# Layer 1's up projection as seven block products over all 1024 tokens, with down after it

## The chip, the cores and the metric

One core of a Trainium2 chip runs the whole program. The metric is the device time of one execution in microseconds. The kernel before took 2512.34, 2510.89 and 2510.45 us in three runs, 2510.89 in the median. Engines are named as in the profile: PE (TensorE), DVE (VectorE), ACT (ScalarE), POOL (GpSimd), SP (SyncE, which issues most transfers).

## The reference, cut to what matters

Two layers over 1024 tokens of width 1024. Each has four token mixers side by side, an output projection and a gated FFN with a causal convolution of three taps over the tokens. All in float32.

```python
def conv_ffn(h, w_up, conv_w, conv_b, w_down):
    a, b = jnp.split(h @ w_up, 2, axis=-1)            # w_up: 1024 x 5632
    a = causal_dwconv(a, conv_w) + conv_b.astype(a.dtype)
    return (jax.nn.gelu(a, approximate=True) * b) @ w_down   # 2816 x 1024

def hybrid_layer(x, ...):
    h = rms_norm(x, g_pre_mix)
    p = h @ w_in
    ...
    y = jnp.concatenate([y_a, y_b, y_c, y_d], axis=-1).astype(dt)   # pool, retention, gating, deltanet
    x = x + rms_norm(y @ w_out, g_post_mix)
    h = rms_norm(x, g_pre_ffn)
    x = x + rms_norm(conv_ffn(h, w_up, conv_w, conv_b, w_down), g_post_ffn)
    return x
```

The deltanet mixer is a recurrence over chunks of 64 tokens: a triangular system is solved in each chunk, then the state is carried on.

## The kernel before

**Numbers.** Every matmul operand is a pair of fp32r tiles: hi, a cast by ACT, and lo, the difference by DVE (`split`, and `unit` for weights, L182 and L183). A product is three matmuls: hi hi, hi lo, lo hi. `a_unit` multiplies one weight tile of 1024 x 128 with the transposed rows of 512 tokens: 8 x 3 = 24 matmuls 512 columns wide (L192 to L194). `b_units` is the form with tokens on the output's partitions, 256 columns wide (L213 to L215).

**Tiling.** The tokens go through in two halves h of 512, each in four blocks of 128. A layer is, for each half, `win` (input projection and mixers), `out` (output projection, then `norms`: the residual and the norm ahead of the FFN), and `ffn`. An FFN has 22 blocks f of 128 channels. For each, two units give the two parts of the up projection, ACT and DVE do the convolution, the gelu and the product (L1020 to L1029), and the result g is split. Two blocks f at a time go through `down`: per token block and half of the output, 6 matmuls and an addition to `acc` in SBUF (L997 to L1004). So up and down alternate through the whole FFN, and neither g nor the transposed rows leave SBUF.

**The end of layer 1.** `out` of half 1 is called in the middle of half 0's `ffn`, after 14 of its 22 blocks f (`MID` = 7). Half 1's normed rows are transposed (`to_hT`), half 1's `ffn` follows, and `last_norm` ends the program.

**Order.** The Tile framework schedules the instructions of each engine ahead of time, from its own model of their times and from priorities, and puts in the waits; each engine then runs its queue strictly in that order. In this way the mixers of half 1 in layer 1 are spread among the matmuls of half 0's FFN. The deltanet's second part is, per block of 128 tokens, `dn_solve` (four steps, each some small matmuls and a copy that the next step needs: L854, L862, L871, L877 with L886 and L888) and `dn_scan` (L916 and L923 carry the state, L931 and L934 make the output, then `heads_norm` and the transposes L940). Transfers are nearly all issued by SP, in its queue's order.

Of the kernel before, what the change touches and what calls it, by code (L numbers as in the profile page):

```python
# [19 lines left out]
P = 128  # L20
# [93 lines left out]

class Net:
    up = 0

    def __init__(self, tc, ctx, t, dbg=None):
# [13 lines left out]
        self.pd = pool("pd", 1, space=DRAM)  # L132
        self.setup()

    def setup(self):
# [146 lines left out]
        return g  # L282

    def sumsq(self, x):
        sq = self.px.tile([P, D], BF16, tag="junk", name="sq", bufs=1)
# [4 lines left out]
    def norms(self, raw, hn, gpost, gpre, src, dst):  # L290
        nc = self.nc
        for b in range(NB):
            xb = self.px.tile([P, D], F32, tag="xb", name="xb")
            nc.sync.dma_start(xb, src[b * P:b * P + P])
            if raw is not None:
                r = self.sumsq(raw[b])
                nc.vector.scalar_tensor_tensor(raw[b], raw[b], r, gpost, ALU.mult, ALU.mult)
                nc.vector.tensor_tensor(xb, xb, raw[b], ALU.add)
                nc.sync.dma_start(dst[b * P:b * P + P], xb)
            if gpre is not None:  # L300
                r = self.sumsq(xb)
                nc.vector.scalar_tensor_tensor(hn[b], xb, r, gpre, ALU.mult, ALU.mult)

    def last_norm(self, raw, gpost, src, dst):
        nc = self.nc
        xbs = []
        for b, tag in enumerate(("qf", "kt", "rg", "su")):
            xb = self.pp.tile([P, D], F32, tag=tag, name=f"x{tag}")
            nc.gpsimd.dma_start(xb, src[b * P:b * P + P])
            xbs.append(xb)  # L310
        V = nc.vector
        mk = lambda nm: self.px.tile([P, 1], F32, tag=f"{nm}1", name=nm, bufs=4)
        for b, xb in enumerate(xbs):
            sq = self.px.tile([P, D], BF16, tag="junk", name="sq", bufs=1)
# [630 lines left out]
    def out(self, l, h, y, mid=False, halves=False):  # L945
        self.up = UO
        nc, t = self.nc, self.t
# [31 lines left out]
        self.norms(raw, hn, gpost, gpre, src, dst)  # L979
        return hn  # L980

    def ffn(self, l, h, hT, mid=None):
        self.up = UF
# [73 lines left out]
    def run(self):  # L1057
# [98 lines left out]
```

## Time and profile before

| | |
|---|---|
| median of three runs | 2510.89 us |
| profiled execution, span | 2507.0 us |
| PE busy | 2447.9 us, 98% |
| DVE busy | 1730.2 us, 69% |
| ACT busy | 943.0 us, 38% |
| POOL busy | 234.0 us, 9% |
| PE's share of the chain of waits | 84% |

The program itself took the span, 2507.0 us, from its first instruction to its last in one execution; the times of the runs are from others, and their median is 3.9 us above it. Stages of layer 1 in that execution: half 1's mixers and half 0's FFN up to about 1914 us, `out` of half 1 from 1914 to 2013 us, half 0's remaining FFN and half 1's from there to 2495 us, and the last norm to 2507 us. In a row of a timeline the first number is the start and the second the duration in us; what stands in brackets is idle time ahead of it and what ended it. In a row of groups the numbers behind the bar are the sum in us and the mean of one in ns. In a row by stretches each engine has its busy time and its count, followed by the granted clock of PE, the share of the DMA engines and GB/s.

### The profile page before, as it was taken

What the parts mean: (1) busy time and instruction counts of PE and PEld (TensorE: products, weight loads), DVE (VectorE), ACT (ScalarE), POOL (GpSimd) and SP (SyncE); (2) the same over time, 40 slices, a digit from 0 to 9 for tenths busy, and PEclk for the clock granted to TensorE, in tenths of its full rate; (3) what the DMA queues carried; (4) which work ended last, traced back from release to release, by engine and by line L of the source; (5) the groups of instructions that cost most, each with busy time, mean ns of one, the idle gap of its engine ahead of it and who ended that gap; (6) DMA issues with size and microseconds to landing.
All of it is one profiled execution on the core that took longest, in us unless ns stands there. A gap on an engine that the chain in (4) does not pass through costs nothing.

```text
span 2507.0 us, 35870 instructions
## 1 busy us (share of the span) xinstructions
PE 2447.9 (98%) x13916; PEld 2035.9 (81%) x13916; DVE 1730.2 (69%) x3561; ACT 943.0 (38%) x1417; POOL 234.0 (9%) x318
## 2 busy tenths in 40 slices
PE   8989998999999999899999999989999999999998
PEld 7968987877788987787778898778778988888886
DVE  8895699765655788956665579895556386555556
ACT  6334452432332454342332345333233343323233
POOL 2321103000000022200000002220000000000001
PEclk9999999999999999999999999999999999999999
DMA  5233333322223452232223354222223253422332
GB/s 186 72 90 111 127 137 91 99 85 76 81 93 113 157 177 76 76 102 78 76 76 101 118 169 160 85 76 85 76 85 101 93 172 114 157 93 87 101 101 84
DMA packets 94655, 265.60 MB, mean 106 GB/s; under 512 B 30146, under 2 KB 30466, under 8 KB 93972
## 3 DMA queue, kind: packets, MB, share of 16 engines
q1 hardware_dynamic: 90564, 251.17, 31.0%
q0 software_dynamic: 3344, 11.08, 1.3%
q8 instruction: 110, 1.80, 0.3%
q10 hardware_dynamic: 576, 1.05, 0.1%
q14 instruction: 61, 0.50, 0.1%
HBM read 241.20 MB, written 22.05 MB: 105 GB/s over the span
## 4 chain that ended last, share of the span: by engine, by line
PE 84%; DVE 11%; issue 4%; ACT 1%; DMA 0%; POOL 0%; SPq 0%; DVEq 0%; POOLq 0%; ACTq 0%
PE psg L193 16%; PE psg L194 16%; PE psg L192 15%; PE psg L997 7%; PE psg L998 6%; PE psg L999 6%; PE psg L213 3%; PE psg L214 3%; PE psg L215 3%; DVE pr L811 3%; DVE A L813 2%; DVE wlo L183 1%; PE psh L345 1%; PE psm L871 1%; PE psm L934 1%
## 5 line engine op out<-in xcount | busy, mean ns | idle before, releaser
L193 PE MATMUL psg<-hT,whi 128*128 128x512 f32 x1856 | 739.1, 398 | 1.8 <-DVE hT L349 1.8
L194 PE MATMUL psg<-hT,wlo 128*128 128x512 f32 x1856 | 737.7, 399 | 0.0
L192 PE MATMUL psg<-hT,whi 128*128 128x512 f32 x1856 | 731.0, 394 | 0.1
L182 ACT CAST whi<-raw 128x1024 fp32r<-128x1024 f32 (+1 forms) x383 | 398.0, 1048 | 782.1 <-PE psg L193 316.2
L183 DVE TENSOR_TENSOR wlo<-raw,whi 128x1024 fp32r<-128x1024 f32 (+1 forms) x360 | 442.2, 1235 | 283.1 <-ACT whi L182 276.0
L192 PEld LDWEIGHTS psg<-hT,whi 128*128 128x128 f32 x1856 | 353.5, 190 | 79.7 <-issue 0.2
L193 PEld LDWEIGHTS psg<-hT,whi 128*128 128x128 f32 x1856 | 349.6, 188 | 83.6 <-DVE hT L349 2.6
L194 PEld LDWEIGHTS psg<-hT,wlo 128*128 128x128 f32 x1856 | 349.5, 188 | 75.6 <-issue 0.2
L1004 DVE TENSOR_TENSOR acc<-acc,psg 128x512 f32<-128x512 f32 x312 | 212.7, 686 | 135.9 <-PE psg L999 134.5
L997 PE MATMUL psg<-whi,g 128*128 128x512 f32 x696 | 277.3, 400 | 0.3 <-DVE acc L1004 0.3
L998 PE MATMUL psg<-wlo,g 128*128 128x512 f32 x696 | 273.9, 394 | 0.0
L999 PE MATMUL psg<-whi,g 128*128 128x512 f32 x696 | 273.4, 393 | 0.0
L214 PE MATMUL psg<-wlo,hT 128*128 128x256 f32 (+1 forms) x512 | 150.0, 294 | 8.4 <-DVE wlo L183 8.4
L997 PEld LDWEIGHTS psg<-whi,g 128*128 128x128 f32 x696 | 130.7, 188 | 31.4 <-DVE acc L1004 1.6
L999 PEld LDWEIGHTS psg<-whi,g 128*128 128x128 f32 x696 | 130.8, 188 | 30.3
L998 PEld LDWEIGHTS psg<-wlo,g 128*128 128x128 f32 x696 | 130.9, 188 | 27.3 <-DVE c L1029 0.2
L1029 DVE TENSOR_TENSOR c<-c,psg 128x512 f32<-128x512 f32 x88 | 60.5, 688 | 131.7 <-PE psg L194 125.0
L215 PE MATMUL psg<-whi,hT 128*128 128x256 f32 (+1 forms) x512 | 149.4, 293 | 0.0
L213 PE MATMUL psg<-whi,hT 128*128 128x256 f32 (+1 forms) x512 | 146.9, 291 | 1.3 <-DVE rqk L490 1.1
L213 PE MATMUL psg<-whi,y 128*128 128x256 f32 x512 | 141.8, 282 | 1.7 <-ACT raw L975 0.9
L215 PE MATMUL psg<-whi,y 128*128 128x256 f32 x512 | 142.8, 282 | 0.0
L214 PE MATMUL psg<-wlo,y 128*128 128x256 f32 x512 | 142.6, 281 | 0.0
(380 smaller groups left out, 3178.9 us busy)
## 6 DMA issues: line engine op xcount, KB each, us to landing
raw<-in_wU SPq DMA_DIRECT2D x176, 512.0 KB, 3.5
raw<-in_wD SPq DMA_DIRECT2D x88, 512.0 KB, 3.5
raw<-in_wA SPq DMA_DIRECT2D x56, 512.0 KB, 3.6
raw<-in_wO SPq DMA_DIRECT2D x32, 512.0 KB, 3.9
raw<-in_wB SPq DMA_DIRECT2D x24, 512.0 KB, 3.5
xs<-xb SPq DMA_DIRECT2D x24, 512.0 KB, 3.4
xb<-xs SPq DMA_DIRECT2D x20, 512.0 KB, 3.6
raw<-in_wS SPq DMA_DIRECT2D x8, 528.0 KB, 3.6
```

Of the source, the lines that this page charges most:

```text
L182: nc.scalar.copy(hi[:, :n], raw[:, :n])
L183: eng.tensor_tensor(lo[:, :n], raw[:, :n], hi[:, :n].bitcast(F32), ALU.subtract)
L192: nc.tensor.matmul(ps, a[0], b[0], start=first, stop=False)
L193: nc.tensor.matmul(ps, a[0], b[1], start=False, stop=False)
L194: nc.tensor.matmul(ps, a[1], b[0], start=False, stop=last)
L213: self.nc.tensor.matmul(ps[:, :width], h0, hi[:, s], start=k == 0, stop=False)
L214: self.nc.tensor.matmul(ps[:, :width], h0, lo[:, s], start=False, stop=False)
L215: self.nc.tensor.matmul(ps[:, :width], h1, hi[:, s], start=False, stop=k == len(hT) - 1)
L997: nc.tensor.matmul(ps, hi[:, tb], us[i][0][:, s], start=i == 0, stop=False)
L998: nc.tensor.matmul(ps, hi[:, tb], us[i][1][:, s], start=False, stop=False)
L999: nc.tensor.matmul(ps, lo[:, tb], us[i][0][:, s], start=False, stop=i == len(g0) - 1)
L1004: V.tensor_tensor(acc[b][:, s], acc[b][:, s], ps, ALU.add)
```

## The change

Only layer 1's FFN and what surrounds it changes (`FULL = (1,)`).

- **Plain part.** For f = 0 to 7, half 0's up projection is made as before (`plain_up`): five blocks ahead of `out` of half 1 and three behind it. g goes to DRAM (`gD`) unsplit.
- **Normed rows to DRAM.** `norms` of layer 1 also writes the normed rows of both halves to DRAM (`hnD`).
- **Three memory layouts.** `phase` closes one set of SBUF pools and opens another: one for the mixers, one for the up projection, one for down.
- **Operands.** `build` reads a half's normed rows back, transposes them, and makes seven operands (hi and lo each) from the four blocks A11, A12, A21, A22 (token half by half of the 1024 channels): A11, A12, A22, S1, S2, S3, Q4.
- **Seven products.** `up_f` loads both weight tiles of a block f, forms seven 512 x 128 weight operands by four additions on DVE (L1111) and seven splits (L1106, L1107), and makes seven products of 4 x 3 = 84 matmuls (L1090 to L1092) in place of eight. Sums of products are kept in PSUM or made by ACT and DVE. For f = 0 to 7 it runs on half 1 alone (256 columns), for f = 8 to 21 on both halves (512 columns). g goes to DRAM.
- **Down.** `down_full` then reads g back and runs over all eight token blocks, in one group of two f and five groups of four. The last group ends each token block with its norm (`end_block`).

A line of the program before is found 18 to 20 lines further down in the changed one up to `dn_scan` (L854 is L874, L862 L882, L871 L891, L877 L897, L886 and L888 L906 and L908, L916 L936, L931 and L934 L951 and L954, L940 L960).

**The tail of the deltanet on PE, before.** The end of one block (L940) and the first two steps of the next (L854, L862); L192 to L194 are half 0's up projection, `x_97` the solve's tile.

```order
L940 MATMUL psm<-ident,tmp 128x128 x2
L854 MATMUL psm<-x_97,LT 32x32 x8
L192 MATMUL psg<-hT_16160,whi 128x512
L193 MATMUL psg<-hT_16162,whi 128x512
L194 MATMUL psg<-hT_16160,wlo 128x512
...
L192 MATMUL psg<-hT_16160,whi 128x512
L862 MATMUL psm<-XT,x_97 32x32 x8
L193 MATMUL psg<-hT_16162,whi 128x512
```

22 matmuls of 512 columns stand between the two steps.

**The same place on PE, after.** The end of one block and the steps of the next.

```order
L954 MATMUL psm<-R_14590,AT 128x64 x2
L960 MATMUL psm<-ident,tmp 128x128 x2
L874 MATMUL psm<-x_100,LT 32x32 x8
L882 MATMUL psm<-XT,x_100 32x32 x8
L891 MATMUL psm<-R_14590,XT 128x128 x4
L897 MATMUL psm<-AT,R_14590 64x128 x4
L906 MATMUL psm<-kt,R_14590 64x64
L908 MATMUL psm<-R_14590,kt 64x64
...
L936 MATMUL psm<-S,tmp 64x64 x8
L951 MATMUL psm<-Sb,qf 64x128 x2
L954 MATMUL psm<-R_14590,AT 128x64 x2
```

The steps now follow one another directly; the up and down matmuls that stood between them have moved behind.

**SP's queue around `build`, after**, with what each row waits for (a name of an engine, or of a transfer queue): g's writes of the plain part (L1026), the last normed rows (L322), the normed rows read back (L1052) and the weights of the first products (L1101).

```order
L1026 DMA gD_109<-c 128x512 [waits DMAHW1_49,DVE_49]
L1101 DMA wraw<-in_wU 128x2x1024 [waits DMAHW2_49,PE_49]
L322 DMA hnD_107<-osu 128x1024 [waits DMAHW3_49,DVE_49]
L1052 DMA hn<-hnD_107 128x1024 [waits DMASW4_49,DMAHW4_49,DMASW2_49,DMASW0_49]
L1052 DMA hn<-hnD_107 128x1024 [waits DMAHW6_49,DMAHW5_49,DMAHW1_49]
L1052 DMA hn<-hnD_107 128x1024 [waits DMASW1_49]
L1052 DMA hn<-hnD_107 128x1024 [waits DMAHW7_49,DMAHW3_49]
```

The rows are read back behind the write of the last of them.

**SP's queue at the start of down, after**: the last writes of g (L1164), g read back (L1177) and the first weights of down (L198).

```order
L1164 DMA gD_109<-c 128x1024 [waits DMAHW4_49,DVE_49,Activation_49]
L1177 DMA graw<-gD_109 128x1024 [waits PE_49]
L1177 DMA graw<-gD_109 128x1024 [waits DMAHW6_49]
L1164 DMA gD_109<-c 128x1024 [waits DMAHW7_49,DVE_49,Activation_49]
L198 DMA raw<-in_wD 128x1024 [waits DMAHW0_49]
L198 DMA raw<-in_wD 128x1024 [waits DMAHW1_49]
```

The first weights of down stand behind the write of the last block's g, which waits for DVE.

The diff, cut to its core:

```diff
+FULL = (1,)
+NPRE, NHALF = 5, 8
...
+    def mix_phase(self):
+        self.phase(("pw", 3), ("pr", NR), ("pa", 4), ("py", 2), ("pt", 5), ("ph", 4), ("pp", 1))
+    def up_phase(self):
+        self.phase(("pv", 2), ("pu", 1), ("pA", 1))
+    def down_phase(self):
+        self.phase(("pw", 6), ("pg", 6), ("pa", 8), ("pr", 2), ("py", 2))
...
                 nc.vector.scalar_tensor_tensor(hn[b], xb, r, gpre, ALU.mult, ALU.mult)
+                if keep is not None:
+                    nc.sync.dma_start(keep[b * P:b * P + P], hn[b])
...
+    def plain_up(self, l, h, fs, hT):
+        for f in fs:
+            c = self.pa.tile([P, HALF], F32, tag="acc", name="c")
+            pa = self.a_unit(self.t["wU"][l, 2 * f], hT)
+            pb = self.a_unit(self.t["wU"][l, 2 * f + 1], hT)
+            with self.tc.high_priority(offset=1500):
+                self.conv_gate(l, h, f, c, pa, pb)
+            self.nc.sync.dma_start(self.gD[l][f, :, h * HALF:h * HALF + HALF], c)
...
+    def build(self, l, h):
...
+            def put(n, src):
+                hi, lo = self.A[n]
+                nc.scalar.copy(hi[:, :, cs], v4(src))
+                V.tensor_tensor(lo[:, :, cs], v4(src), hi[:, :, cs].bitcast(F32), ALU.subtract)
+            put("A11", p00)
+            nc.scalar.copy(a21, p10)
+            V.tensor_tensor(s1, a21, p11, ALU.subtract)
+            put("S1", s1)
+            V.tensor_tensor(s2, s1, p00, ALU.subtract)
+            put("S2", s2)
+            put("A12", p01)
+            V.tensor_tensor(s3, p00, a21, ALU.subtract)
+            put("S3", s3)
+            V.tensor_tensor(q4, s2, p01, ALU.add)
+            put("Q4", q4)
+            put("A22", p11)
...
+    def up_f(self, l, f, halves):
...
+        self.product(X, "A11", w11, cs, True, False)
+        self.product(Z, "S1", wt1, cs, True, False)
+            nc.scalar.copy(p1, X)
+            nc.scalar.copy(p5, Z)
+        self.product(X, "S2", wt2, cs, False, False)
+        self.product(W, "A12", w21, cs, True, True)
+            nc.scalar.copy(u2, X)
+            V.tensor_tensor(p1, p1, W, ALU.add)
+        self.product(X, "S3", wt3, cs, False, False)
+        self.product(Z, "Q4", w22, cs, False, True)
+            V.tensor_tensor(at[:, :, 1], v(p5), v(X), ALU.subtract)
+            V.tensor_tensor(at[:, :, 0], v(Z), v(u2), ALU.subtract)
+        self.product(X, "A22", wt4, cs, False, True)
+            nc.scalar.activation(c, a[:, 2:], AF.Identity, bias=cb, scale=w(2))
...
+        nc.sync.dma_start(self.gD[l][f, :, halves[0] * HALF:halves[0] * HALF + 2 * N], c)
...
-        acc = self.ffn(l, 0, self.to_hT(acc, True), lambda: hn.extend(self.out(l, 1, y, True)))
-        hT = self.to_hT(hn)
-        self.ffn_norm(l, 0, acc)
-        self.ffn_norm(l, 1, self.ffn(l, 1, hT))
+        hT = self.to_hT(acc, True)
+        self.plain_up(l, 0, range(NPRE), hT)
+        self.out(l, 1, y, True)
+        self.plain_up(l, 0, range(NPRE, NHALF), hT)
+        self.up_phase()
+        self.rows(l)
+        self.build(l, 1)
+        for f in range(NHALF):
+            if f == 1:
+                self.build(l, 0)
+            self.up_f(l, f, (1,))
+        for f in range(NHALF, NF):
+            self.up_f(l, f, (0, 1))
+        self.down_phase()
+        self.down_full(l)
```

More of the change, by code (lines that the diff above doesn't have):

```diff
@@ L143, in setup @@
         self.xs = [self.pd.tile([SEQ, D], F32, name=f"xs{i}") for i in range(2 * DEPTH - 1)]
+        self.hnD = [self.pd.tile([SEQ, D], F32, name=f"hnD{i}") for i in range(DEPTH)]
+        self.gD = [self.pd.tile([NF, P, SEQ], F32, name=f"gD{i}") for i in range(DEPTH)]
         self.pm = {}
@@ L288, in sumsq, with norms @@
         return self.rstd(ss, 1, 1.0 / D)
-    def norms(self, raw, hn, gpost, gpre, src, dst):
+    def norms(self, raw, hn, gpost, gpre, src, dst, keep=None):
         nc = self.nc
         for b in range(NB):
-            xb = self.px.tile([P, D], F32, tag="xb", name="xb")
+            xb = self.py.tile([P, D], F32, tag="xb", name="xb")
             nc.sync.dma_start(xb, src[b * P:b * P + P])
@@ L978, in out, with conv_gate @@
         hn = raw if mid else self.acc_tiles()
-        self.norms(raw, hn, gpost, gpre, src, dst)
+        self.norms(raw, hn, gpost, gpre, src, dst, self.hnD[l][h * HALF:h * HALF + HALF] if l in FULL else None)
         return hn
+    def conv_gate(self, l, h, f, c, pa, pb):
+        nc, pf = self.nc, self.pf[l]
+        V, cf = nc.vector, self.state[l]["cf"]
+        w = lambda j: pf[:, PF_CW + 3 * f + j:PF_CW + 3 * f + j + 1]
+        cb = pf[:, PF_CB + f:PF_CB + f + 1]
+        nc.scalar.activation(c, pa, AF.Identity, bias=cb, scale=w(2))
+        if h == 0:
+            nc.scalar.copy(cf[:, f, :], pa[:, 510:512])
+        V.scalar_tensor_tensor(c[:, 1:512], pa[:, 0:511], w(1), c[:, 1:512], ALU.mult, ALU.add)
+        V.scalar_tensor_tensor(c[:, 2:512], pa[:, 0:510], w(0), c[:, 2:512], ALU.mult, ALU.add)
+        if h == 1:
+            V.scalar_tensor_tensor(c[:, 0:2], cf[:, f, :], w(0), c[:, 0:2], ALU.mult, ALU.add)
+            V.scalar_tensor_tensor(c[:, 0:1], cf[:, f, 1:2], w(1), c[:, 0:1], ALU.mult, ALU.add)
+        nc.scalar.activation(c, c, AF.Gelu_apprx_tanh)
+        V.tensor_tensor(c, c, pb, ALU.mult)
@@ new lines, in product @@
+    def product(self, ps, a, b, cs, first, last):
+        nc = self.nc
+        ah, al = self.A[a]
+        for k in range(4):
+            s = slice(k * P, k * P + P)
+            st, sk = first and k == 0, not first
+            nc.tensor.matmul(ps, b[:, 0, s], ah[:, k, cs], start=st, stop=False, skip_group_check=sk)
+            nc.tensor.matmul(ps, b[:, 0, s], al[:, k, cs], start=False, stop=False, skip_group_check=sk)
+            nc.tensor.matmul(ps, b[:, 1, s], ah[:, k, cs], start=False, stop=k == 3, skip_group_check=sk)
@@ new lines, in down_full @@
+    def down_full(self, l):
+        nc, t = self.nc, self.t
+        V = nc.vector
+        gpost = self.bcast(t["gB"][4 * l + 3], "gpost", pool=lambda n: self.py.tile([P, D], F32, tag="gpost", name=n, bufs=1))
+        acc = [self.pa.tile([P, D], F32, tag="acc", name=f"acc{b}") for b in range(2 * NB)]
+        groups = [[0, 1]] + [list(range(f, f + 4)) for f in range(2, NF, 4)]
+        for fs in groups:
+            us, gs = [], []
+            for f in fs:
+                us.append(self.unit(t["wD"][l, f]))
+                r = self.r4("graw")
+                nc.sync.dma_start(r, self.gD[l][f])
+                g = self.pg.tile([P, 2, SEQ], F32R, tag="g", name="g")
+                with self.tc.high_priority(offset=2000):
+                    self.split(g[:, 0], g[:, 1], r)
+                gs.append(g)
+            last = fs is groups[-1]
+            for b in range(2 * NB):
+                tb = slice(b * P, b * P + P)
+                for n in range(2):
+                    s = slice(n * 512, n * 512 + 512)
+                    ps = self.ps() if n else self.pq()
+                    for i in range(len(fs)):
+                        g, u = gs[i], us[i]
+                        nc.tensor.matmul(ps, g[:, 0, tb], u[0][:, s], start=i == 0, stop=False)
+                        nc.tensor.matmul(ps, g[:, 0, tb], u[1][:, s], start=False, stop=False)
+                        nc.tensor.matmul(ps, g[:, 1, tb], u[0][:, s], start=False, stop=i == len(fs) - 1)
+                    with self.tc.high_priority(offset=1500):
+                        if fs[0] == 0:
+                            nc.scalar.copy(acc[b][:, s], ps)
+                        else:
+                            V.tensor_tensor(acc[b][:, s], acc[b][:, s], ps, ALU.add)
+                if last:
+                    with self.tc.high_priority(offset=1500):
+                        self.end_block(l, b, acc[b], gpost)
@@ new lines, in end_block @@
+    def end_block(self, l, b, acc, gpost):
+        nc = self.nc
+        V = nc.vector
+        rows = slice(b * P, b * P + P)
+        xb = self.py.tile([P, D], F32, tag="xb", name="xb")
+        nc.gpsimd.dma_start(xb, self.xs[2 * l][rows])
+        mk = lambda nm: self.px.tile([P, 1], F32, tag=f"{nm}1", name=nm, bufs=4)
+        sq = self.py.tile([P, D], BF16, tag="junk", name="sq", bufs=1)
+        ss = self.px.tile([P, 2], F32, tag="ss2", name="ss2", bufs=4)
+        g = self.py.tile([P, D], F32, tag="gx", name="gx")
+        for n in range(2):
+            s = slice(n * 512, n * 512 + 512)
+            nc.scalar.activation(sq[:, s], acc[:, s], AF.Square, accum_out=ss[:, n:n + 1])
+            (nc.gpsimd if n == 0 else V).tensor_tensor(g[:, s], acc[:, s], gpost[:, s], ALU.mult)
+        r, t, v = mk("rs"), mk("rt"), mk("rv")
+        V.tensor_scalar(v, ss[:, 0:1], 1.0 / D, EPS, ALU.mult, ALU.add)
+        V.scalar_tensor_tensor(v, ss[:, 1:2], 1.0 / D, v, ALU.mult, ALU.add)
+        self.rsqrt(r, v, t)
+        for n in range(2):
+            s = slice(n * 512, n * 512 + 512)
+            V.scalar_tensor_tensor(xb[:, s], g[:, s], r, xb[:, s], ALU.mult, ALU.add)
+            nc.sync.dma_start(self.t["out"][rows, s], xb[:, s])
```

111 lines of the change are left out of this document (100 added, 11 removed).

## The prediction

> **What bounds the kernel now.** I read the busy shares and the chain of waits first, then the stages of layer 1 as stretches of the span.
>
> ```profile
> PE 2447.9 (98%) x13916; PEld 2035.9 (81%) x13916; DVE 1730.2 (69%) x3561; ACT 943.0 (38%) x1417; POOL 234.0 (9%) x318
> PE 84%; DVE 11%; issue 4%; ACT 1%; DMA 0%; POOL 0%; SPq 0%; DVEq 0%; POOLq 0%; ACTq 0%
> ...
> core 0: us, PE busy (x) PEld busy (x) DVE busy (x) ACT busy (x) POOL busy (x), PEclk, DMA share, GB/s
> 1756.00:1914.00 158.00, 158.00 (x1021) 124.80 (x1020) 95.75 (x181) 51.23 (x86) 8.15 (x25) 1.00 0.25 81
> 1914.00:2013.00 99.00, 99.00 (x618) 88.85 (x618) 44.81 (x62) 30.99 (x48) 0.54 (x1) 1.00 0.30 96
> 2013.00:2110.00 97.00, 97.00 (x429) 79.02 (x428) 70.98 (x145) 39.52 (x60) 1.39 (x3) 1.00 0.46 152
> 2110.00:2495.00 385.00, 384.68 (x1669) 312.55 (x1668) 227.23 (x368) 127.59 (x167) 7.88 (x9) 1.00 0.32 104
> ...
> 418.00:431.00 13.00, 10.50 (x46) 8.78 (x47) 12.79 (x22) 3.28 (x7) 0.00 (x0) 0.61 0.26 81
> ```
>
> The chain of waits is TensorE for 84%. From 1756 to 2495 us (layer 1's FFN with the tail of half 1's mixers and its output projection in it) PE is busy without a hole at clock 1.00, VectorE only 45 to 73%. The tail of the deltanet, out's norms and the splits of the weights all lie under matmuls there. So a matmul removed is time gained, and work that loses its cover is time lost. The last row is an early stretch with a busy VectorE and holes in PE: its granted clock is 0.61.
>
> **The matmuls.** The steps from one start to the next:
>
> ```profile
> 2299.69 0.40 PE L193 MATMUL psg<-hT,whi 128*128 128x512 f32 x1
> 2311.95 0.39 PE L997 MATMUL psg<-whi,g 128*128 128x512 f32 x1
> ...
> 1999.77 0.28 PE L215 MATMUL psg<-whi,y 128*128 128x256 f32 x1
> 2006.58 0.28 PE L215 MATMUL psg<-whi,y 128*128 128x256 f32 x1
> ...
> 1469.79 0.87 PE psh L345 x8
> ```
>
> Between the first two lie 53 steps of 512 columns: 12.26/53 = 0.2313 us each. Between the next two 58 steps of 256 columns: 6.81/58 = 0.1174 us. Eight transposes take 0.87 us, 0.109 each. For a block f over both halves, before does 4 units x 24 = 96 matmuls of 512; the seven products need 7 x 4 x 3 = 84: 12 x 0.2313 = 2.78 us less, for 14 blocks -38.9. For f = 0 to 7, half 1 alone takes 84 matmuls of 256 in place of 48 of 512: 9.86 against 11.10, -1.24 each, -9.9 in all. Half 0's plain units and down's 1056 matmuls stay. Added are 32 net transposes, +3.5. Matmuls: **-45.3**.
>
> [...]
>
> **The deltanet tail loses its cover (D).** On PE's queue in the changed kernel, half 1's deltanet blocks 1 to 3 stand one after another with no other matmul between their steps (excerpts above); before, up or down matmuls lie between them, 22 between the first two. Only ten plain units come ahead of out. A bare block lasts as long as its chain, whose steps are:
>
> ```profile
> 1795.54 0.45 PE L854 MATMUL psm<-x,LT 128*32 128x32 f32 x16
> 1796.32 0.30 DVE L857 COPY x<-psm 32x128 f32<-32x128 f32 x1 [0.19 <-ACT x L857]
> 1801.26 0.45 PE L862 MATMUL psm<-XT,x 128*32 128x32 f32 x16
> 1801.89 0.53 ACT L866 ACTIVATE XT<-psm 32x128 f32<-32x128 f32 x2
> 1806.38 1.05 PE L871 MATMUL psm<-R,XT 128*128 128x128 f32 x8
> 1807.60 0.68 DVE L872 TENSOR_TENSOR R<-psm,Dv 128x512 f32<-128x512 f32 x1
> 1811.51 0.66 PE L877 MATMUL psm<-AT,R 128*64 128x128 f32 x8
> 1812.86 0.67 ACT L892 COPY tmp<-psm 128x256 f32<-128x256 f32 x2 [7.64 <-PE psm L888]
> 1822.65 0.45 PE L916 MATMUL psm<-S,tmp 64*64 64x64 f32 x8
> 1823.03 0.44 PE L931 MATMUL psm<-Sb,qf 128*64 128x128 f32 x4
> 1823.15 0.29 DVE L923 TENSOR_TENSOR S<-S,psm 128x128 f32<-128x128 f32 x1 [1.70 <-PE psm L916]
> 1824.36 0.66 PE L934 MATMUL psm<-R,AT 128*128 128x64 f32 x4
> ...
> L588 ACT ACTIVATE tmp<-psm 128x256 f32<-128x256 f32 x4 | 1.5, 385 | 16.6 <-PE psm L934 16.6
> L590 DVE TENSOR_REDUCE hs<-tmp 128x4 f32<-128x256 f32 x4 | 1.7, 420 | 6.4 <-ACT tmp L588 6.4
> L264 DVE TENSOR_TENSOR rt<-rt,hs 128x4 f32<-128x4 f32 x4 | 0.6, 161 | 0.1
> L597 DVE TENSOR_TENSOR tmp<-psm,rs 128x256 f32<-128x256 f32 x4 | 1.7, 423 | 0.2
> ```
>
> Read from the start of a step's matmul to the end of the copy that the next one needs: L854 to the end of L857 1.1, L862 to L866 1.2, L871 to L872 1.9, L877 to L892 2.0 (the sixteen small products in between included). Then L916 to L923 0.8, a second L916 0.4, L931 and L934 2.0 (1823.03 to 1825.02). The heads norm: 0.4 + 0.4, ten tiny ones at 0.16 and a gap, some 1.9, and 0.4, with the handovers 3.4. The transposes 0.4. Together 13.2, with handovers that cover now hides 13.5. PE's own part, by the durations above, is about 6.5, which it pays before as well; so 7.0 idle a block, 21 for three. Block 4 has the first of out's matmuls among it: half, 4 (a choice between 0 and 7). The last retention block ends in the same norm: 5. And a PE busy for half the time gets the clock of the row 418:431 rather than 1.00: some 25 us of PE work at 0.61 would be 16 longer; part of it shortens holes, so I take 12. **D = +42**, bounds 26 (block 4 covered, clock kept) and 58 (every handover 0.2 us longer, clock fully lost).
>
> [...]
>
> **The second norms and the memory switch (N).**
>
> ```profile
> 2012.80 0.28 PE L215 MATMUL psg<-whi,y 128*128 128x256 f32 x1
> ...
> 2017.94 1.28 DVE L302 SCALAR_TENSOR_TENSOR oqf<-xb,rs,oap 128x1024 f32<-128x1024 f32 x1
> 2058.24 1.28 DVE L302 SCALAR_TENSOR_TENSOR osu<-xb,rs,oap 128x1024 f32<-128x1024 f32 x1
> ...
> L183 DVE TENSOR_TENSOR wlo<-raw,whi 128x1024 fp32r<-128x1024 f32 x18 | 21.9, 1223 | 12.8 <-ACT whi L182 12.4
> L182 ACT CAST whi<-raw 128x1024 fp32r<-128x1024 f32 x17 | 17.7, 1050 | 39.5 <-PE psg L193 16.9 <-PE psg L999 16.0 <-DMA raw<-in_wU 6.5
> L1004 DVE TENSOR_TENSOR acc<-acc,psg 128x512 f32<-128x512 f32 x20 | 13.6, 684 | 4.9 <-PE psg L999 4.8
> L1024 DVE SCALAR_TENSOR_TENSOR c<-psg,pf,c 128x510 f32<-128x510 f32 x6 | 4.5, 749 | 0.1
> L1020 ACT ACTIVATE c<-psg,pf 128x512 f32<-128x512 f32 x6 | 4.6, 774 | 0.5 <-PE psg L194 0.5
> L1028 ACT ACTIVATE c<-c 128x512 f32<-128x512 f32 x6 | 3.8, 632 | 8.8 <-DVE c L1024 8.8
> ...
> raw<-in_wD SPq DMA_DIRECT2D x88, 512.0 KB, 3.5
> ```
>
> Count from out's last matmul as t = 0. Before, the normed rows are done at t = 6 to 47, under down matmuls. Now six plain units follow, 6 x 24 x 0.2313 = 33.3 us of cover. With little else on VectorE I put the last row at t = 40. It goes to DRAM and comes back through SP, 3.5 and 3.5 by the DMA row, and SP holds the weight loads and g's writes in the same order; transposes, the first cast and subtract, and the first product starts at t = 54.
>
> From there VectorE is the bound. A half block has 7 subtracts and 4 adds of 128x512 at 0.61 to 0.68 (half of L183's, L1004's), 7.2 us; its epilogue is three 256 wide ones at about 0.35 on PSUM, two steps of 512 at 0.75 and two products at 0.35: 3.3. That is 10.5 against PE's 9.86. The operands of two halves add 4 x 11 of 128x512, 29 us, of which 7 come before the first product. 8 x 10.0 (epilogues of the last reach past it) + 22 = 102: half blocks end at t = 156. PE needs 33.3 + 8 x 9.86 + 7 (64 transposes) = 119 to 122. **N = +34**; bounds 20 (rows at t = 32, all subtracts at 0.60) and 56 (rows at t = 47, handovers on top).
>
> **The full blocks (U).** For 19.4 us of PE a block has 11 subtracts and adds (7.2) and 1024 wide epilogues (three of 0.69, two of 1.5, two of 0.69: 6.5), 13.7 on VectorE; ScalarE 7 casts of 0.53 and about 4.5. Both fit: **0**, bounds 0 and 4, should three PSUM buffers hold back a product.
>
> **The start of down (T).** Before, down and up alternate. Now all of g comes first. Behind the last Q4 product stand a subtract 0.7, L1020's kind at 1024 columns 1.4, two of L1024's kind 2.8, L1028's kind 1.1, two products 1.4: 7.4, of which the last product's 12 x 0.2313 = 2.8 is covered. On SP g's last write waits for that, and the first two loads of down weights are issued behind it (excerpt above): 4.6 + 0.7 + 3.5 landing + 1.05 cast and part of the subtract = **+10.5**, bounds 8 and 15. Later loads hide under 22 us of group work. The end is as before, a norm of one block (-1 to +3); writing normed rows of half 0 costs SP four issues, nothing (0 to 4) while PE has the next projection.
>
> **Sum**: -45.3 + 42 + 34 + 0 + 10.5 = +41 on the span of 2507.0: 2548. The median of the runs, 2510.89, is 3.9 above that span, so **2552**. A measurement of this kernel tells about 0.2% (5 us) from no change.
>
> **Rivals.** *Short waits*: D, N and T at their low bounds, 26 + 20 + 8 = 54 against 45.3, +9: 2520. For it: much of D and N are estimates of handovers. Against: the order has the rows bare. *Not slower*: the mechanism is that successive deltanet blocks overlap more than the chain says, since a solve does not need the previous block's state. Then the norm of one block runs beside the next solve, a block costs 3 to 4 idle rather than 7 and holds the clock: D = 10, with N and T at their low bounds 38 in all, -7: 2504. It decides from D + N + T under 45. Against: PE takes its queue in order, and the transposes that need the norm stand ahead of the next L854. *The clock falls through the half blocks too*: with VectorE as bound, PE has holes as in 418:431; at twice the step a half block takes 84 x 0.235 = 19.7 us, for five of them +50: 2602. Against: 94% busy is denser than that row. That the products don't save what they say would need another step at 256 columns than 0.117, and the row shows it.
>
> **Chances.** Forecast (near 2552) 0.58; short waits 0.17; not slower 0.17, of it 0.12 faster and 0.05 within 0.2%; clock 0.08. So faster 0.12, same 0.05, slower 0.83. The range 2517 to 2590 takes in the short waits, and most of the bounds of D, N and T.
>
> **What would show it.** Right: around 1700 to 1790 us PE busy near half with idle ended by DVE and ACT at the lines of the solve and of the heads norm; a hole of about 20 us after the plain units ended by a DMA of normed rows; VectorE over 95% busy in the half blocks; full blocks every 19.4 us; one hole of 10 us at down's first weights. Wrong: bare blocks every 10 us or less, the first product within 5 us of the last plain unit, or full blocks above 20 us, which would add 14 times the excess.

## The result and the profile after

The changed kernel takes 2571.68 us (median of four runs, 2569.47 to 2573.77) against 2511.54 us: 1.024 times as long, 95% interval 1.0225 to 1.0254. The profiled execution spans 2570.5 us, 63.5 more than before. Forecast were 2552 us and slower, with a range of 2517 to 2590.

The busy shares of the page after, and its clock in 40 slices of the span:

```profile
PE 2444.2 (95%) x14068; PEld 2041.1 (79%) x14068; DVE 1771.3 (69%) x3665; ACT 963.6 (37%) x1505; POOL 242.7 (9%) x343
PEclk9999999999999999999999999995899999999999
```

PE was busy for 98% before and is for 95%. Its busy sum hardly falls, though there are fewer columns to multiply, in good part because one slice in 40 ran at about half clock, where the same work takes longer (four matmuls of L954 1.12 us at clock 0.50 and 0.66 at 1.00). The chain of waits, which carried the first part of the prediction, is of no use here: followed back from the end it stops after 1% of the span, at the transfers of the last residual rows.

The same stages as before, in stretches (columns: busy time and count of PE, weight load, DVE, ACT, POOL, then granted clock, DMA share, GB/s). They are: up to the end of out of half 1; plain units, norms, `build` and half blocks; full blocks; down.

```profile
1663.00:1866.00 203.00, 169.95 (x1217) 145.23 (x1214) 100.22 (x234) 54.06 (x98) 9.84 (x27) 0.81 0.21 64
1866.00:2024.40 158.40, 130.75 (x881) 120.81 (x880) 140.16 (x284) 84.59 (x158) 3.58 (x9) 0.94 0.42 153
2024.40:2298.70 274.30, 273.49 (x1177) 219.68 (x1175) 176.78 (x248) 109.43 (x165) 2.88 (x16) 1.00 0.21 78
2309.00:2556.00 247.00, 247.00 (x1056) 199.41 (x1056) 126.10 (x209) 59.44 (x85) 12.33 (x12) 0.99 0.31 104
```

The first two stretches are where the time went: 203 us at a mean clock of 0.81, and 158 us in which VectorE is the busiest engine. The full blocks and down have next to no hole.

Set against before, with 0.2313 us for a matmul of 512 columns on both sides:

| stage | measured | forecast |
|---|---|---|
| up to out's end: 202.6 less 5 up blocks, against 349.9 less 16 up and 14 down blocks | +52.5 | +42 |
| full blocks: 274.3 against 14 x 22.2 | -36.5 | -38.9 |
| out's end to the first full block: 158.4 against 33.3 + 8 x 11.10, less 4.9 of transposes and holes before | +31.4 | +27.6 (34 + 3.5 - 9.9) |
| hole ahead of down | +10.2 | +10.5 |
| down's 1056 matmuls: 247.4 against 244.3 | +3.1 | 0 |
| after the last matmul: 14.2 against 11.6 | +2.6 | 0 |
| sum | +63.3 | +41.2 |

The bare tail of the deltanet, by short stretches and in PE's timeline:

```profile
1744.00:1746.00 2.00, 0.00 (x0) 0.00 (x0) 1.79 (x9) 0.16 (x1) 0.00 (x0) 1.00 0.25 96
1746.00:1748.00 2.00, 0.64 (x4) 0.31 (x4) 1.07 (x5) 0.00 (x0) 0.00 (x0) 0.71 0.00 0
1748.00:1765.00 17.00, 10.88 (x113) 8.63 (x112) 5.89 (x22) 1.92 (x6) 2.21 (x8) 0.50 0.01 2
1783.00:1801.00 18.00, 11.91 (x122) 9.01 (x122) 5.98 (x23) 1.92 (x6) 1.81 (x6) 0.50 0.00 1
1814.00:1816.00 2.00, 2.00 (x15) 2.00 (x14) 0.48 (x2) 0.00 (x0) 0.59 (x2) 0.73 0.00 0
...
1747.36 0.69 PE L680 MATMUL psm<-ident,tmp 128*128 128x128 f32 x2 [3.62 <-DVE tmp L617]
1760.51 1.12 PE L954 MATMUL psm<-R,AT 128*128 128x64 f32 x4
1765.12 0.69 PE L960 MATMUL psm<-ident,tmp 128*128 128x128 f32 x2 [3.50 <-DVE tmp L617]
1765.74 0.64 PE L874 MATMUL psm<-x,LT 128*32 128x32 f32 x16
```

The clock falls in the norm's hole of the last retention block (1743.7 to 1747.4) and stays at 0.50 until about 1815: three deltanet blocks, and 14 of the 24 us of the fourth, at half clock. Block starts (L874) are at 1748.0, 1765.7, 1783.3 and 1800.8, 17.6 us apart. Each of the first three has one hole of 3.5 us for its norm and four of 0.5 to 0.8, 6.1 us in all.

### The profile page after: what moved, and what is told of

Same layout as the page of the kernel before. It is cut to its first block, busy times and chain, and to the rows that moved or that the text cites. A ratio compares the mean times of both kernels' runs of the same rounds, so it can differ in the third digit from the quotient of the medians.

```text
span 2570.5 us, 36403 instructions
## 1 busy us (share of the span) xinstructions
PE 2444.2 (95%) x14068; PEld 2041.1 (79%) x14068; DVE 1771.3 (69%) x3665; ACT 963.6 (37%) x1505; POOL 242.7 (9%) x343
## 5 line engine op out<-in xcount | busy, mean ns | idle before, releaser
L211 PE MATMUL psg<-hT,whi 128*128 128x512 f32 x1280 | 509.1, 398 | 1.3 <-DVE hT L369 1.3
L210 PE MATMUL psg<-hT,whi 128*128 128x512 f32 x1280 | 508.9, 398 | 0.5 <-DVE hT L369 0.3
L212 PE MATMUL psg<-hT,wlo 128*128 128x512 f32 x1280 | 508.9, 399 | 0.0
L201 DVE TENSOR_TENSOR wlo<-raw,whi 128x1024 fp32r<-128x1024 f32 (+1 forms) x267 | 329.6, 1240 | 180.1 <-ACT whi L200 175.3
L211 PEld LDWEIGHTS psg<-hT,whi 128*128 128x128 f32 x1280 | 241.7, 189 | 57.1 <-DVE hT L369 1.9
L212 PEld LDWEIGHTS psg<-hT,wlo 128*128 128x128 f32 x1280 | 241.8, 189 | 55.8 <-issue 0.2
L210 PEld LDWEIGHTS psg<-hT,whi 128*128 128x128 f32 x1280 | 241.6, 189 | 54.8 <-ACT hT L368 0.6
L1247 DVE TENSOR_TENSOR acc<-acc,psg 128x512 f32<-128x512 f32 x160 | 109.1, 686 | 74.6 <-PE psg L1242 74.0
L1106 ACT CAST w<-wraw 128x512 fp32r<-128x512 f32 x154 | 92.2, 619 | 138.3 <-PE psg L1092 57.7
L1240 PE MATMUL psg<-whi,g 128*128 128x512 f32 x352 | 141.5, 404 | 0.0
L1241 PE MATMUL psg<-wlo,g 128*128 128x512 f32 x352 | 138.8, 394 | 0.0
L1242 PE MATMUL psg<-whi,g 128*128 128x512 f32 x352 | 138.6, 394 | 0.0
L1107 DVE TENSOR_TENSOR w<-wraw,w 128x512 fp32r<-128x512 f32 x154 | 103.6, 688 | 46.5 <-ACT w L1106 45.3
L831 DVE SCALAR_TENSOR_TENSOR pr<-A 64x1 f32<-64x1 f32 (+30 forms) x124 | 115.2, 929 | 5.6 <-POOL A L827 3.6
```

Source lines behind the costliest of these rows:

```text
L201: eng.tensor_tensor(lo[:, :n], raw[:, :n], hi[:, :n].bitcast(F32), ALU.subtract)
L210: nc.tensor.matmul(ps, a[0], b[0], start=first, stop=False)
L211: nc.tensor.matmul(ps, a[0], b[1], start=False, stop=False)
L212: nc.tensor.matmul(ps, a[1], b[0], start=False, stop=last)
L831: V.scalar_tensor_tensor(pr[:, 0:i, 0:i], A[:, 0:i, 0:i], -1.0, A[:, 0:i, i].unsqueeze(1).to_broadcast([64, i, i]), ALU.mult, ALU.mult)
L1240: nc.tensor.matmul(ps, hi[:, tb], us[i][0][:, s], start=i == 0, stop=False)
```

## The experiments

Theory after the result: the products save what they should (about 2.7 us a full block), and the rest is the uncovered tail at half clock, VectorE in the half blocks, and the late start of down. Each part is undone or measured alone. All are changes to the changed kernel, and times stand against its 2571.7.

**Give the tail its cover back.**

```diff
-NPRE, NHALF = 5, 8
+NPRE, NHALF = 18, 21
```

> 18 plain blocks of half 0 ahead of out instead of 5, and 3 behind it as before (21 half blocks, one full block). On PE's queue up matmuls now stand between all steps of the last retention block and of all four deltanet blocks. Theory (the tail lost its cover, D is about 49 us from 1739 to 1825 us): that stretch has no PE idle beyond 2 us and the clock stays above 0.95; 13 blocks f move from 19.6 us to 11.1 + about 10.5, which costs 26; so 2572 - 47 + 26 = about 2551 (2543 to 2562). Rival (the tail is slow for another reason than the missing matmuls): idle and clock stay, 2572 + 26 = about 2598.

Measured: 2553.4 us (2550.95 and 2555.92). A stretch of one deltanet block in this run:

```profile
1808.00:1848.00 40.00, 40.00 (x248) 31.49 (x246) 18.92 (x37) 12.21 (x21) 2.12 (x8) 1.00 0.31 97
```

PE has no hole and clock 1.00. Out ends 100.4 us later than in the changed kernel, although 13 x 11.10 = 144.3 us of plain units were put ahead of it: the lost cover cost 43.9 us (48 without the 4 us that this execution lost earlier, in layer 0). In the long run of half blocks each takes 10.54 us; so a block f, plain for one half and by products for the other, takes 21.6 instead of 19.60. That is the price of this cover, and why only 18 us remain of 44.

**More plain units behind out.**

```diff
-NPRE, NHALF = 5, 8
+NPRE, NHALF = 5, 13
```

> 5 plain blocks ahead of out as in the change, but 8 behind it instead of 3 (13 half blocks): 89 us of plain units over the norms and the reading back of the rows. It tells how N (39 us) divides. If N is the wait for the rows that the plain units do not cover, the 12 us hole ahead of the first transposes and most of the 23 us lost in the first two half blocks go; five blocks f cost 2 each more: 2572 - 30 + 10 = about 2552. If the lost time in the first half blocks is VectorE's work on operands and weights, which cannot start before its memory is free, only the hole goes: 2572 - 13 + 10 = about 2569. If nothing goes, 2582.

Measured: 2579.2 us, near the case in which nothing goes. From the last plain unit to the first product it is 13.3 us, against 18.0 in the changed kernel, and the first two half blocks still take 42.6. What SP's queue waited for from 1940 to 1962 us:

```profile
SPq L1026 <- DVE c L1016: 16.9, 2, 10.8
SPq L1052 <- DMA gD<-c: 1.2, 1, 1.2
```

The rows (L1052) had been in DRAM for some 45 us, but their reads stand behind the write of the last plain g and wait for that transfer too. Whether the queue or the memory holds them is tried further down.

**Keep PE busy in the short holes.** `warm` issues useless matmuls of 512 columns into the step's own PSUM tile: 4 ahead of each step of the solve, 3 for each state and 2 for the output.

```diff
-        pw = self.pq(src)
+        pw = self.warm(self.pq(src), 4)
```

> The change with useless matmuls of 512 columns (22 for a deltanet block of half 1 in layer 1, 5.1 us at full clock) ahead of the steps' own ones, into the same PSUM tile, which the real ones then overwrite; the order of the real ones is the same, and the norm's hole of 3.9 us stays. Theory (the half clock in the bare stretch costs some 4 of the 17.6 us of a block): granted clock above 0.9 there, a block 14 to 15 us, in all 10 to 14 us less than 2572: about 2560. Rival (the clock falls whatever fills the short holes, since the norm's hole is still there, or it costs nothing): 17.6 us or more a block, up to 20, and 2572 to 2582.

Measured: 2577.2 us, no gain; blocks start 18.8 to 20.0 us apart. Around one norm's hole:

```profile
1756.00:1764.00 8.00, 7.22 (x86) 5.17 (x84) 2.76 (x8) 0.67 (x2) 0.66 (x2) 1.00 0.02 5
1764.00:1766.00 2.00, 0.49 (x4) 0.35 (x4) 0.90 (x4) 0.38 (x1) 1.15 (x4) 1.00 0.02 4
1766.00:1768.00 2.00, 0.01 (x1) 0.02 (x1) 1.58 (x9) 0.00 (x0) 0.00 (x0) 0.57 0.00 0
1768.00:1772.00 4.00, 4.00 (x25) 2.90 (x26) 0.78 (x2) 0.26 (x1) 0.00 (x0) 0.50 0.00 0
1772.00:1776.00 4.00, 4.00 (x33) 3.13 (x32) 0.00 (x0) 0.54 (x2) 0.40 (x2) 0.86 0.05 7
```

The clock now does come back, and falls again at each norm: here it is 0.50 from 1766.26 us, 1.8 us into the norm's hole, to 1773.09, after 5.1 us of dense work. The useless matmuls cost as much as the clock gave, so this run does not say what the clock is worth.

**Let a block's norm run beside the next solve.** In `dn_back`, for this half only: three steps of a block's solve are written ahead of the transposes of the previous block.

```diff
-            for x, y in zip(A_, B_):
-                turns([x, y], 1)
+            late = None
+            for x, y in zip(A_, B_):
+                for _ in range(3):
+                    next(x)
+                if late is not None:
+                    turns([late], 1)
+                next(x)
+                turns([x], 1)
+                for _ in range(3):
+                    next(y)
+                late = y
+            turns([late], 1)
```

> The change with the deltanet's blocks of that half written in another order: the norm of a block runs beside the first three steps of the next one's solve, and its transposes come behind them. Theory (a bare block lasts as long as its chain, 3.9 us of it the norm's hole): 4 us less for three blocks, 13.5 instead of 17.6 us each, 2572 - 12 = about 2560. Rival (another limit, such as the PSUM buffers that the next solve waits for): less than 1 us a block, 2569 to 2572.

Measured: 2560.3 us, but the two times lie far apart (2554.51 and 2566.14), and the profiled execution is some 6 us late already in layer 0. So the tail is read from the trace: from the same up matmul near 1714 us to out's end it takes 137.6 us, in the changed kernel 152.5 (in x_clock 157.5). Blocks start 10.7 (the first one's next solve was pulled ahead), 14.2 and 14.2 us apart. One block of it, and the transposes behind the norm:

```profile
1766.00:1780.00 14.00, 11.67 (x116) 8.96 (x114) 5.89 (x22) 1.92 (x6) 2.20 (x8) 0.50 0.02 4
1773.86 0.66 PE L974 MATMUL psm<-ident,tmp 128*128 128x128 f32 x2 [1.21 <-DVE tmp L618]
```

The norm's hole shrinks from 3.5 to 1.2 us, and with it two of the short holes close: PE is idle for 2.3 us of a block instead of 6.1. The gain is 3.4 us for each later block where 4 were expected, and a little at the first. But the clock is still 0.50, and now PE itself, busy for 11.7 of 14 us at half speed, is most of what a block takes.

**Keep the clock from falling in the first place.** On top of that order, 20 useless transposes of the squares fill the hole of the last retention block's norm, where the clock had fallen.

```diff
+            if self.tail and b == NB - 1:
+                for i in range(20):
+                    nc.tensor.transpose(pT[:, i % 2 * P:i % 2 * P + P], self.sq[:, i % 2 * P:i % 2 * P + P], self.ident)
```

> The reordered blocks of x_overlap, and 20 useless transposes of the squares (2.2 us at full clock) in the hole of the last retention block's norm, in which the clock fell to 0.50 about 3 us after PE's last matmul and then stayed there for 65 us. Theory (the clock falls after some 3 us without a matmul and needs a dense stretch of 4 to 5 us to come back, so keeping that one hole short keeps it up through the holes of at most 1.2 us that are left): clock 1.00 from 1740 us on, a block about 10 us instead of 14.2, 2560 - 16 = about 2544. Rival (a half busy PE loses its clock whatever the holes): clock back at 0.50, 14 us a block, 2558 to 2562.

Measured: 2548.8 us (2547.37 to 2550.66), 11.5 below x_overlap's middle, where 16 were expected; the same stretch takes 130.1 us. The clock holds at the retention's norm and for one block, and falls later:

```profile
1756.00:1760.00 4.00, 3.35 (x51) 2.73 (x46) 1.49 (x7) 1.12 (x4) 1.54 (x6) 1.00 0.05 11
1760.00:1762.00 2.00, 0.31 (x3) 0.11 (x2) 1.79 (x8) 0.00 (x0) 0.00 (x0) 1.00 0.05 7
1762.00:1763.00 1.00, 0.76 (x10) 0.62 (x10) 0.41 (x2) 0.00 (x0) 0.00 (x0) 1.00 0.00 0
1763.00:1768.00 5.00, 4.52 (x73) 3.43 (x68) 2.21 (x8) 0.74 (x2) 0.65 (x2) 0.50 0.02 5
```

At full clock PE reaches the transposes earlier, so the norm's hole is longer there, 1.9 us, with one of 0.65 us shortly ahead of it; behind the two the clock is 0.50 again. So the first half of the theory stands (the next blocks start 7.9, 11.5 and 14.2 us apart), and here the clock fell behind holes of 0.65 and 1.9 us (more on this in the last section).

**Down's first weights on another queue, and a third buffer at the end.**

```diff
-                us.append(self.unit(t["wD"][l, f]))
+                us.append(self.unit(t["wD"][l, f], q=nc.gpsimd if fs[0] == 0 else None))
...
-        self.phase(("pw", 6), ("pg", 6), ("pa", 8), ("pr", 2), ("py", 2))
+        self.phase(("pw", 6), ("pg", 6), ("pa", 8), ("pr", 2), ("py", 3))
```

> The change with down's first two weight tiles issued on GpSimd's queue, so that they do not stand behind the write of the last g on SP's, and a third buffer for the residual rows at the end. Theory (T of 10.2 us is 4.6 of epilogue and then the landing of weights that were issued too late): the hole ahead of down's first matmul 5 to 6 us; the end 14.2 to about 11.6; 2572 - 7 = about 2565. Rival (the loads wait for something else as well, such as the memory of the up phase, or g's splits end no sooner): 10 us stay, 2569.

Measured: 2567.0 us. First the start of down in the changed kernel, then in this run (ACT's casts of g and of the weights):

```profile
2302.24 0.69 DVE L1163 TENSOR_TENSOR c<-c,psg 128x512 f32<-128x512 f32 x1
2302.99 0.32 SPq L1164 DMA_DIRECT2D gD<-c  x1
2303.35 1.20 SPq L198 DMA_DIRECT2D raw<-in_wD  x2
2307.80 1.04 ACT L200 CAST whi<-raw 128x1024 fp32r<-128x1024 f32 x1 [4.51 <-DMA raw<-in_wD]
```

```profile
2300.66 1.04 ACT L205 CAST g<-graw 128x1024 fp32r<-128x1024 f32 x1 [0.95 <-DMA graw<-gD]
2303.08 1.04 ACT L205 CAST g<-graw 128x1024 fp32r<-128x1024 f32 x1 [1.37 <-DMA graw<-gD]
2304.03 1.99 ACT L200 CAST whi<-raw 128x1024 fp32r<-128x1024 f32 x2
```

The hole is 8.2 us instead of 10.2. The weights no longer wait on SP, but their casts stand behind those of g on ACT, and the second g's rows land only at 2303. The end falls from 14.2 to 11.2 us: with two buffers the last residual rows could be read only once an earlier block's output had left,

```profile
POOL xb L1207 <- DMA out<-xb: 8.4, 4, 3.1
```

as this row of the changed kernel's waits says.

**Move VectorE's additions and subtracts to GpSimd.** Four additions of weights in each half block, and the subtracts of S1, S2, S3 and Q4 in `build`.

```diff
-            V.tensor_tensor(raw[:, o], raw[:, o], raw[:, a], ALU.add)
+            (nc.gpsimd if n == 1 else V).tensor_tensor(raw[:, o], raw[:, o], raw[:, a], ALU.add)
```

> The change with the four weight additions of each half block and 16 of the 28 subtracts of the operands moved from VectorE to GpSimd. Theory (from the first product to the last half block VectorE is the bound): 0.69 us less for each of the 48 on VectorE's queue there, so the 107 us from the first product to the first full block fall towards PE's 8 x 9.97 + 7 = 87; given GpSimd's 1.26 us each, 8 to 14 us less, 2558 to 2564. Rival (the first two half blocks wait for rows and buffers on SP's queue rather than for VectorE, or GpSimd slows VectorE down): less than 3 us, or a loss.

Measured: 2576.3 us, a loss, as the rival had it. The groups of the half blocks, in the changed kernel and then in this run:

```profile
L1107 DVE TENSOR_TENSOR w<-wraw,w 128x512 fp32r<-128x512 f32 x51 | 33.7, 686 | 3.5 <-ACT w L1106 2.8
L1159 DVE SCALAR_TENSOR_TENSOR c<-a,pf,c 128x512 f32<-128x512 f32 x8 | 6.0, 748 | 1.5 <-issue 1.5
```

```profile
L1107 DVE TENSOR_TENSOR w<-wraw,w 128x512 fp32r<-128x512 f32 x51 | 41.4, 841 | 11.7 <-ACT w L1106 11.1
L1111 POOL TENSOR_TENSOR wraw<-wraw 128x512 f32<-128x512 f32 x28 | 40.2, 1436 | 37.0 <-DVE w L1107 36.7
L1159 DVE SCALAR_TENSOR_TENSOR c<-a,pf,c 128x512 f32<-128x512 f32 x8 | 8.3, 1039 | 3.6 <-ACT c L1158 3.6
```

An addition takes GpSimd 1.44 us against VectorE's 0.69, and with GpSimd at work beside it VectorE's own subtracts slow down from 686 to 841 ns and its two-operand steps from 748 to 1039. The run moved the load to a slower chain, so it leaves open whether VectorE was the bound.

**Undo the seven products alone.** Same phases, layouts and transfers, but eight plain block products: four operands, four splits of weights, no additions.

```diff
-        self.product(X, "A11", w11, cs, True, False)
-        self.product(Z, "S1", wt1, cs, True, False)
...
+        self.product(X, "A11", wa0, cs, True, False)
+        self.product(X, "A12", wa1, cs, False, True)
+        self.product(Z, "A21", wa0, cs, True, False)
+        self.product(Z, "A22", wa1, cs, False, True)
```

> The change with its phases, memory layouts and transfers, but eight plain block products in place of the seven: four operands, four weight splits, no additions, 96 matmuls a block. It tells what the seven products are worth here. Theory (2.8 us for each of 14 full blocks, nothing for the half blocks, where VectorE eats the gain): full blocks 22.4 us instead of 19.6, +39; the first product to the first full block about 100 us instead of 107; 2572 + 39 - 8 = about 2603. Rival (the products' gain is lost elsewhere, in PSUM waits or at a lower clock): less than 2590.

Measured: 2597.1 us; with the seven products it is 25 us less. First the half blocks of the changed kernel (the first two, the next three, the last three), then of this run (the first two, the other six):

```profile
1917.00:1960.60 43.60, 30.22 (x204) 28.53 (x205) 39.40 (x67) 25.47 (x49) 0.37 (x2) 0.88 0.26 92
1960.60:1990.50 29.90, 29.90 (x254) 29.90 (x253) 26.95 (x52) 16.13 (x33) 2.08 (x3) 1.00 0.30 111
1990.50:2024.40 33.90, 32.69 (x254) 31.16 (x253) 31.27 (x57) 18.79 (x38) 0.94 (x3) 1.00 0.39 136
```

```profile
1918.00:1947.20 29.20, 28.01 (x233) 27.43 (x234) 14.17 (x24) 11.43 (x21) 0.37 (x2) 1.00 0.51 185
1947.20:2015.50 68.30, 68.30 (x578) 68.30 (x577) 36.33 (x61) 27.92 (x46) 1.95 (x7) 1.00 0.38 124
```

A full block takes 22.31 us by eight products and 19.60 by seven: 14 x 2.71 = 38. The eight half blocks, with `build` among the first two, take 97.5 us by eight and 107.4 by seven: the products cost 10 there. All of that loss lies in the first two (43.6 against 29.2); in the other six the seven products gain, 63.8 against 68.3. Down starts 3.5 us sooner after the last product, whose epilogue is shorter. So 38 - 10 - 3.5 = 24.5, about as timed. In the first two half blocks VectorE works 39.4 of 43.6 us with seven products, and 14.2 of 29.2 with eight. That supports VectorE as the bound of these two, by work left out rather than moved.

**All holes of the tail filled, with x_wd's two edits.** x_keep, and 8 useless transposes in each deltanet norm's hole.

```diff
+        if self.tail and b < NB - 1:
+            for i in range(8):
+                nc.tensor.transpose(pT[:, i % 2 * P:i % 2 * P + P], sq[:, i % 2 * P:i % 2 * P + P], self.ident)
```

> x_keep with 8 useless transposes of the squares also in each deltanet norm's hole (in x_keep the clock held until two holes of 0.65 and 1.93 us came within 4 us), and the early weights and third buffer of x_wd. Theory (short holes keep the clock): clock 1.00 from 1740 us to out, blocks about 10 us instead of 11.5 and 14.2; out ends 8 us earlier than in x_keep (1845 to 1837); down starts 2 and the program ends 3 us earlier: 2549 - 8 - 5 = about 2536. Rival (the useless transposes hold back the real ones as in x_clock, or the clock falls at the holes of 0.8 us): out ends at 1845 or later, 2544 to 2550.

Measured: 2535.9 us (2535.01 to 2537.36), on the forecast. One block of the tail:

```profile
1756.00:1766.00 10.00, 8.19 (x137) 6.47 (x138) 6.07 (x23) 1.79 (x6) 2.21 (x9) 1.00 0.03 6
```

Clock 1.00 throughout with holes of 0.5 to 1.2 us; blocks 7.8, 9.8 and 9.9 us apart; the stretch to out's end takes 121.6 us. Order and clock together are worth 31 us of the tail's 44 to 48 (152.5 less 121.6), without any cover. It is the fastest form of the change here, and still 1.0096 times the kernel before (1.0079 to 1.0113).

**The rows through GpSimd's queue**, first alone, then with 5 plain blocks behind out instead of 3.

```diff
-                nc.sync.dma_start(x[:, :D], self.hnD[l][r0:r0 + P])
+                nc.gpsimd.dma_start(x[:, :D], self.hnD[l][r0:r0 + P])
```

> y_keep2 with the normed rows read back through GpSimd's queue instead of SP's. Theory (in the first two half blocks, 43 us instead of 20, VectorE's work is the bound, and half 1's rows come straight behind their write anyway): hole ahead of the first transposes 12 us as before, first two half blocks 40 to 43 us, 0 to 3 us less than y_keep2. Rival (the transposes of half 0's rows, which SP issued 21 us late behind weights, hold PE's queue): first two half blocks under 35 us, 8 us or more less.

> y_rows8 with 5 plain blocks behind out instead of 3 (10 half blocks). In x_behind five more plain blocks did not help, since SP issued the reads of the rows only behind the last plain g. Theory (the hole ahead of the first product is that queue and the norms' length): last plain unit to first product 6 us instead of 18, two blocks cost 2 each: 8 us less than y_rows8, about 2527. Rival (the hole is the memory switch: the rows' buffers come free only with the last plain unit): 13 us as in x_behind, no gain.

Measured: 2541.8 and 2540.1 us, no gain either time (y_keep2 2535.9). The first two half blocks take 43.1 us in both, so half 0's rows on SP were not what held them. From the last plain unit to the first product it is 17.9 and 12.3 us, about as in the changed kernel and in x_behind. From y_rows10, a wait of GpSimd's queue, then the timeline of PE and ACT behind the last plain unit, which ends at 1890.4 us:

```profile
POOL hn L1074 <- DMA gD<-c: 10.2, 1, 10.2
...
1890.16 0.62 ACT L1128 CAST w<-wraw 128x512 fp32r<-128x512 f32 x1 [2.14 <-PE psg L212]
1890.19 0.60 PE L1082 MATMUL psg<-ident,hn 128*128 128x128 f32 x4
1896.78 0.57 ACT L1089 CAST A11h<-psg 128x512 fp32r<-128x512 f32 x1
1900.56 1.11 PE L1082 MATMUL psg<-ident,hn 128*128 128x128 f32 x4 [7.58 <-ACT a L1094]
```

On a queue that holds no write of g, the reads still wait for one, so it was not SP's queue alone that tied them; that their buffers lie where the plain phase keeps g is the likely reason. But in y_rows10 PE does not wait for the rows any more: the first transposes (L1082) stand directly behind the last plain unit. ACT's first cast of the products' weights (L1128) waits for a matmul of that unit, six such casts stand ahead of the first operand's (L1089), and PE waits 7.6 us for ACT. So the number that the rival gave came out, and not by its mechanism: with the rows there in time, making the first weights and operands on ACT and VectorE takes as long. Another order of that work, or another place in memory, was not tried.

## Why the prediction was right, and where its sizes were off

**The matmuls: right.** 19.60 us a full block against 19.43, and x_plain shows the saving by itself, 2.71 against 2.78.

**D: mechanism right, one term small.** x_full shows the cause: with cover the stretch has no hole, at clock 1.00, and 44 to 48 us come back against 42 forecast. Blocks 1 to 3 came out as 3 x (17.6 - 6.5) = 33, the sum of the 21 of idle and 12 of clock. That it agrees so well is partly luck, since the split was not as told: the clock was 0.50 and not 0.61, from one hole in the retention's norm on, and with 6.1 us idle in each block, 18 of the 33 are idle and 15 are matmuls that took longer. With the clock kept a block takes 9.8 us in y_keep2's order; in the changed kernel's own order no run shows it at full clock. The last retention block took 8.8 us, near the 4 of work and 5 of hole. The term that failed is block 4's "half, 4": from its start to the last of its waits 24.2 us pass, of which 6.5 are its own and 6.3 are 54 matmuls of out; 11 remain. The rest of the 52.5, some 3 us beyond these, lies in the stretch of the transposes ahead of the tail (12.7 us from the same matmul to the first plain unit, against 8.0 before) and was not looked into.

On the clock the prediction drew its 12 us from the row at 0.61, whose PE is 81% busy. From the hole of 3.6 us on the clock was lower, 0.50 for 68 us. PE's busy share does not explain that: y_keep2's tail is busy for 8.2 of 10 us, about as in that row, and has 1.00. Nor was PE idle throughout ahead of every fall: in x_keep the clock fell behind 3.41 us in which PE was busy for 1.48. By what rule it falls and returns no run shows (last section).

**N: right in time.** Forecast were the first product at t = 54 and the last half block at 156 after out's end; measured 51.1 and 158.4. A half block bound by VectorE was put at 10.5 us and takes 10.54 in x_full's long run:

```profile
2115.00:2220.40 105.40, 104.98 (x842) 100.89 (x840) 99.67 (x181) 59.98 (x121) 6.62 (x10) 1.00 0.38 125
```

VectorE is busy for 95% there, but PE has no hole either, so which of the two binds is not settled. In the changed kernel's half blocks VectorE is busy for 91% (97.6 of 107.4 us), where over 95% were to show it: the first two take 43.6 us and the other six 10.6 on average, so the time agrees and its spread does not. Why the first product is late was partly wrong: behind 3 plain blocks it is the norms' length and the two transfers, but more cover would not have helped beyond 5 to 6 us, since the first weights and operands are then still to be made (y_rows10).

**T: right in size, its lever wrong.** 10.2 against 10.5. The load behind the last g was named as the cause; without it 8.2 remain, since g's own rows and casts are as late.

**What was put at nothing** adds up to 8 us: full blocks 0.17 us longer each (2.4), down at 0.234 us a matmul (3.1), and the end, where a third buffer gives back 3.0.

**The rivals.** *Short waits* fell: the first two waits came out above the forecast, and the third 0.3 us below it. *Not slower* named a mechanism that exists (x_overlap: blocks do overlap, when they are written so), but the order it was judged by did not have it. *The clock falls through the half blocks* fell: 0.88 in the first two, 1.00 in the rest.

## What to carry to other kernels

Count what a saved matmul had been hiding: these products are worth 38 us in the full blocks and 25 us in all, and the order that they need uncovered 44 us of a serial tail. When such a tail stands bare, its order and the filling of its holes (for the clock) were worth 31 us here, more than the cover that could be bought back with plain blocks at 2 us each. Where an engine that is nearly full must build the operands at the same time, a smaller product count on TensorE was no gain here: in the two half blocks that share VectorE with `build` the seven products lost 14 us to eight, and in the other six, also at 256 columns, they gained 4.5.

## What was not expected of the hardware

- In the norms' holes the clock fell after different times. In the changed kernel it was 0.50 from 1746.82 to 1815.09 us; in x_clock from 1766.26 to 1773.09, and again from about 1786.8 to 1793.6. From PE's last matmul to the fall it took 3.1 us in the changed kernel, and 1.8 and 2.7 behind the first two deltanet blocks of x_clock. The return there came after 5.1 and 6.1 us of dense work. With four holes of 0.5 to 0.8 us and one of 3.5 in each 17.6 us it did not come back for 68 us.
- PE was not idle throughout ahead of every fall. The last 3.41 us ahead of one in x_keep and of one in y_rows8, and as long a stretch of y_keep2, behind which the clock stayed at 1.00:

```profile
1759.59:1763.00 3.41, 1.48 (x17) 1.14 (x15) 2.54 (x11) 0.00 (x0) 0.00 (x0) 1.00 0.05 8
1751.87:1755.28 3.41, 2.15 (x49) 1.62 (x48) 1.79 (x5) 0.67 (x2) 0.00 (x0) 1.00 0.00 1
1748.74:1752.15 3.41, 1.97 (x26) 1.53 (x26) 1.52 (x4) 0.76 (x3) 0.40 (x2) 1.00 0.06 10
```

- This is not settled: PE's busy share alone does not tell these apart, since 2.15 us of 3.41 lost the clock and 1.97 kept it. y_rows8 has the same order of matmuls as y_keep2 and PE busy for 8.17 us from 1750 to 1760, and its clock was 0.50 from 1755.28 to 1765.52, 10.2 us. So that y_keep2's tail keeps its clock may be partly luck.
- In x_pool, where GpSimd made additions (1.44 us each), VectorE's instructions of the same shapes took 23% (686 to 841 ns) and 39% (748 to 1039 ns) longer than in the changed kernel.
